# Attention scores and values accumulated in place by narrower matmuls, in a float32 decoder layer with compensated products

## The chip, the cores and the metric

The kernel runs on one core of one Trainium2 chip. The metric is the device time in microseconds of one execution. The core's engines run side by side, each with its own queue: TensorE (PE in the profile, with its weight loads as PEld), VectorE (DVE), ScalarE (ACT), GpSimd (POOL) and SyncE (SP), which here only starts transfers.

## The reference

A decoder layer for 256 tokens of 2048 channels in float32. The input is normalised and projected; one branch is causal attention with 16 heads and low-rank queries, keys and values, the other a short gated convolution; both are projected, merged by gates, projected once more and normalised. The part that the change touches is the attention:

```python
def one_block(args):
    qn, qr, blk = args                      # a block of 128 queries
    sc = (einsum('bqhd,bkhd->bhqk', qn, k_nope)
          + einsum('bqhr,bkr->bhqk', qr, k_rope)).astype(float32) * scale
    mask = key_pos[None, :] <= q_pos[:, None]
    sc = where(mask[None, None], sc, -inf)
    p = softmax(sc, axis=-1).astype(v.dtype)
    return einsum('bhqk,bkhd->bqhd', p, v)
...
attn = attn.reshape(b, s, MLA_WIDTH) * silu(z_mla)
```

A head has 128 channels without rotary position and 64 with, 128 value channels, 256 queries and keys.

## The kernel before, in words

Float32 products are made of two rounded parts each. An operand is split into a high part in the `fp32r` format (ScalarE copies it, `hi`) and the rest (VectorE subtracts, `lo`), which is `split_act`; a product is then hi x hi + hi x lo + lo x hi, three matmuls into one accumulator (`product`, `products`). Weights come from memory in units of 128 x 2048 (`raw`, three buffers), are split in halves of 1024 columns into `whi` and `wlo` (five buffers each), and are used by TensorE in a fixed order. Every matmul goes through a helper on line 88, so all matmuls have that line in the profile; they are told apart by the tiles they write and read.

The kernel has three stages: the latent products (`qa`, `ckv`, `kr`) up to about 50 us, the loop over 16 heads up to about 590 us, and the square products (`sq`, `sX`, `sY`, `sZ`, `out`) after it. In the loop over heads TensorE mostly works on the big input projections: `z` (the gates, `gates`) and `cv` (the convolution's four projections, `channels`), whose matmuls are 512 columns wide. Between their quarters the heads' own steps are put by hand: `group_a` and `group_r` make queries and keys for two heads (`qn`, `kn`, `qr`), `group_v` the values for four (`vv`), `score(h)` the scores, `turn` the transposed and split weights of the softmax (`pt`), and `values(h)` the weighted sum.

The order of all matmuls is pinned (`tc.keep_in_program_order`). The other engines' instructions are ordered by a planner that simulates a timeline, unless they are pinned too. Accumulators are banks of 128 x 512 float32: a ring of four with the tag `mm`, two with the tag `cv`, one `st`, one `o`.

*Scores before.* `sc` (bank `st`) holds the first block of 128 queries against the first 128 keys, `sw` (a bank `mm`) the second block against all 256. A matmul of the high query part multiplies the high and the low key part side by side in one instruction, so each bank has two halves: the left one collects hi x hi, lo x hi and the high part of the rotary product, the right one hi x lo and the low part of the rotary product (`qr` has its high and low part on the two halves of the partitions). Columns of the six matmuls: 256, 128, 256 for `sc`, and 512, 256, 512 for `sw`. `softmax` has ScalarE copy the two right halves out (`sc_half`, `half`, line 695), VectorE add them to the left ones (lines 698 and 700) and add the causal mask (lines 699 and 701). Then come maximum, exponential, sum and scaling, and a transpose through memory (`turned`: `far<-via` and back). With `behind`, which is given for every second head (`score(h + 1, later=True)`), the copies of line 695 are pinned.

*Values before.* `o` has two halves in the same way. One matmul of 512 columns stands ahead of a `yield`, at which the caller puts other steps, and three of 256, 128 and 256 behind it. `whole` (lines 433 and 434) has ScalarE copy the right half out and VectorE add it to the left; line 745 multiplies the sum into the gate `at`.

Of the kernel before, what the change touches and what calls it, by code (L numbers as in the profile page):

```python
# [14 lines left out]
AF = mybir.ActivationFunctionType  # L15
ALU = mybir.AluOpType
PSUM = bass.MemoryType.PSUM

P = 128
S = 256  # L20
NT = S // P
# [61 lines left out]
def tile_layer(ctx: ExitStack, tc: tile.TileContext, xw, w0, xb, x, pos, pvec, post_g, wc, wz, wcv, wkr, wqk, wqr, wv, cwr, wsq, out):  # L83
    nc = tc.nc
# [151 lines left out]
    def bank(name, tag="mm", bufs=4):  # L236
        return psum.tile([P, 512], F32, name=name, tag=tag, bufs=bufs)
# [94 lines left out]
    kr = bp.tile([P, 2, S], F32R, name="kr")  # L332
    mask = bp.tile([P, 3 * P], F32, name="mask")
# [12 lines left out]
    def temp(name, shape=(P, S), dt=F32, bufs=2, tag=None):  # L346

        tag, n = tag or name.rstrip("0123456789_"), shape[-1]
        if n % LINE == 0:
            return bp.tile(list(shape), dt, name=name, tag=tag, bufs=bufs)  # L350
        return bp.tile([P, -(-n // LINE) * LINE], dt, name=name, tag=tag, bufs=bufs)[:, :n]


    def turned(src, via, n, far=None, queue=nc.gpsimd):

        via = via[:, : P * n]
        v = via.rearrange("p (q k x) -> p q k x", q=4, k=n)
        nc.vector.transpose(v.rearrange("p q k x -> p k q x"), src)  # L358
        if far is None:
            far = dram.tile([P, P * n], F32, name="far", tag=f"far{n}", bufs=4)[:, :]  # L360

        def go():
            f = far.rearrange("(q y) (i m) -> i y q m", q=4, i=4)
            for i in range(4):
                m = via[32 * i : 32 * i + 32, :].rearrange("y (q m) -> y q m", q=4)
                tc.keep_in_program_order(queue.dma_start(out=f[i], in_=m))  # L366

        def come(dst):

            tc.keep_in_program_order(queue.dma_start(out=dst, in_=far))  # L370

        return go, come
# [57 lines left out]
    def whole(dst, ps):  # L430

        t = temp("half")
        nc.scalar.activation(t[:, :], ps[:, S:], AF.Copy)
        nc.vector.tensor_tensor(dst, ps[:, :S], t[:, :], op=ALU.add)
# [237 lines left out]
    def scores(h):  # L672

        (qn, kn), qr = groups["a", h // HG], groups["r", h // HG]
        j = h % HG
        sc, wide_sc = bank(f"sc{h}", tag="st", bufs=1), bank(f"sw{h}")
        t0, t1 = slice(0, P), slice(P, S)
        mm = matmul
        o = sc[:, :S].rearrange("p (i k) -> p i k", i=2)
        mm(o, qn[0][:, j, t0], kn[:, :, j, :P], start=True, stop=False)  # L680
        mm(sc[:, :P], qn[1][:, j, t0], kn[:, 0, j, :P], start=False, stop=False)
        mm(o, qr[:, j, t0], kr[:, :, :P], start=False, stop=True)
        o = wide_sc[:, :].rearrange("p (i k) -> p i k", i=2)
        mm(o, qn[0][:, j, t1], kn[:, :, j, :], start=True, stop=False)
        mm(wide_sc[:, :S], qn[1][:, j, t1], kn[:, 0, j, :], start=False, stop=False)
        mm(o, qr[:, j, t1], kr[:, :, :], start=False, stop=True)
        return lambda behind: softmax(h, sc, wide_sc, behind)

    def softmax(h, sc, wide_sc, behind):
        if h == 0:  # L690
            temp("pad", (P, 4 * LINE), bufs=1)
        p = temp("p", (P, 3 * P), bufs=2)
        half, wide_half = temp("sc_half", (P, P), bufs=1), temp("half")
        for dst, src in ((half, sc[:, P:S]), (wide_half, wide_sc[:, S:])):
            now = nc.scalar.activation(dst[:, :], src, AF.Copy)
            if behind:
                tc.keep_in_program_order(now)
        nc.vector.tensor_tensor(p[:, :P], sc[:, :P], half[:, :], op=ALU.add)
        nc.vector.tensor_tensor(p[:, :P], p[:, :P], mask[:, :P], op=ALU.add)
        nc.vector.tensor_tensor(p[:, P:], wide_sc[:, :S], wide_half[:, :], op=ALU.add)  # L700
        nc.vector.tensor_tensor(p[:, P:], p[:, P:], mask[:, P:], op=ALU.add)
        mx, sm, rs = temp("mx", (P, NT)), temp("sm", (P, NT)), temp("rs", (P, NT))
        nb = temp("nb", (P, NT))
        for t in range(NT):
            o = slice(t * P, (2 * t + 1) * P)
            nc.vector.reduce_max(mx[:, t : t + 1], p[:, o], axis=mybir.AxisListType.X)
        nc.vector.tensor_scalar(nb[:, :], mx[:, :], -SCALE, None, op0=ALU.mult)
        for t in range(NT):
            o = slice(t * P, (2 * t + 1) * P)
            nc.scalar.activation(  # L710
                p[:, o], p[:, o], AF.Exp, bias=nb[:, t : t + 1], scale=SCALE,
                accum_out=sm[:, t : t + 1],
            )
        nc.vector.reciprocal(rs[:, :], sm[:, :])
        for t in range(NT):
            o = slice(t * P, (2 * t + 1) * P)
            nc.vector.tensor_scalar(p[:, o], p[:, o], rs[:, t : t + 1], None, op0=ALU.mult)
        go, come = turned(p[:, :], temp("via", (P, 3 * P), bufs=1), 3)
        go()
        return p, lambda: come(p[:, :])  # L720

    def turn(p):

        pt = temp("pt", (P, 2, 3 * P), F32R, 1)
        hi, lo = (pt[:, j : j + 1, :].rearrange("p o (k q) -> p (o k) q", k=3) for j in range(2))
        split_act(quarters(hi), quarters(lo), by_rows(p[:, :], 3), True)
        return pt

    def values(h, pt):
        vv = groups["v", h // HV]  # L730
        j = h % HV
        o = bank(f"o{h}", tag="o", bufs=1)
        vs = slice(j * DV, (j + 1) * DV)
        both = o[:, :].rearrange("p (i q) -> p i q", i=2)
        mm = matmul
        mm(both, vv[0][:, 0, vs], pt[:, :, :S], start=True, stop=False)
        yield
        mm(o[:, :S], vv[1][:, 0, vs], pt[:, 0, :S], start=False, stop=False)
        mm(o[:, P:S], vv[1][:, 1, vs], pt[:, 0, S:], start=False, stop=False)
        mm(both[:, :, P:], vv[0][:, 1, vs], pt[:, :, S:], start=False, stop=True)  # L740

        at = at_t[:, h // HV, :, :].rearrange("p t (i k x) -> p t i k x", i=4, k=HV)[:, :, :, j, :]
        f = temp("f")
        whole(f[:, :], o)
        nc.vector.tensor_tensor(at, f[:, :].rearrange("p (t i x) -> p t i x", t=NT, i=4), at, op=ALU.mult)


    at_t = at_f[:, :, :].rearrange("p (v t k) s -> p v t (k s)", v=NV, t=NT)
# [188 lines left out]
    def score(h, later=False):  # L937
        made_here = scores(h)

        def rest():  # L940
            ps_by_head[h], come = made_here(later)
            coming.append(come)

        return rest if later else rest()
# [49 lines left out]
    for h in range(H):  # L994
        v, at = divmod(h, HV)
# [12 lines left out]
        if at == 0:  # L1008
            for i in range(4):
                gates(v, i)  # L1010
                if v == 0 and i == 0:
                    ckv_come()
                elif v == 0 and i == 1:
                    key_rope()
                elif v == 0 and i == 2:
                    latent_split("qa", qa, "q_g")
                elif v and i == 0:
                    arrive()
                elif v and i == 1:
                    pt = turn(ps_by_head.pop(h - 1))  # L1020
                elif v and i == 2:
                    o = values(h - 1, pt)
                    next(o)
                    finish_all(make("v", v))
                    score(h)
                    finish_all(o)
                elif v and i == 3:
                    next(tap)
            if not v:
                latent_split("ckv", ckv, "kv_g")  # L1030
            gates_done(v)
            if v:
                arrive()
# [23 lines left out]
        else:  # L1057
            pt = turn(ps_by_head.pop(h - 1))
# [19 lines left out]
        if at:  # L1078
            steps.append(values(h - 1, pt))
# [10 lines left out]
        if h == H - 1:  # L1090
            pt = turn(ps_by_head.pop(h))
# [70 lines left out]
    seq, pending, now = [], {}, [0]  # L1162
# [49 lines left out]
    def branch_block(c, both, n, combine):  # L1212

        sums_of[n, c] = []

        def last(pss):
            for t in range(NT):
                sums_of[n, c].append(pss[t])
                meet((n, c), t, combine)

        return block(c, n, lambda k: both[k // 4][:, k % 4, :], {}, last)
# [147 lines left out]
    p = [branch_block(c, at_b, 2, weigh) for c in range(4)]  # L1369
# [121 lines left out]
    op = ctx.enter_context(tc.tile_pool(name="op", bufs=1))  # L1491
# [177 lines left out]
```

## Time and profile before

| | |
|---|---|
| median of 3 runs | 1013.3 us (1013.11 to 1013.71) |
| span of the profiled execution | 1011.8 us, first to last instruction |
| its time outside the span | not listed; the runs' median is 1.5 us longer than the span |
| TensorE busy | 1004.2 us, 4552 matmuls and 4552 weight loads |
| VectorE busy | 811.4 us, 1111 instructions |
| ScalarE busy | 586.3 us, 838 instructions |
| GpSimd busy | 170.7 us, 311 instructions |
| transfers | 261.84 MB, mean 259 GB/s |
| mean granted TensorE clock | 0.998 |

The profile is one execution, recorded by the hardware. An engine's busy time is the union of its instructions; for matmuls, which overlap, the ends are modelled, so that consecutive starts tell more than lengths. The chain of waits is the work that ended last, followed back from the last instruction through whatever released each step. A row of the groups gives line, engine, operation, output and inputs, the shape, the count, the busy time, the mean length in ns, and the idle time of the engine ahead of them with what ended it.

### The profile page before, as it was taken

The numbers are of one execution on the slowest core, as the hardware profiler recorded it, in microseconds if no ns is written. First come the engines' busy times: TensorE is split into PE (matmuls) and PEld (weight loads), VectorE is DVE, ScalarE is ACT, GpSimd is POOL, SyncE is SP. The second block draws the span as 40 slices with busy tenths as digits, with TensorE's granted clock in tenths as the row PEclk, the third lists the DMA queues.
The fourth block names the chain that finished last, engine by engine and source line by source line (L and its number), as shares of the span: only waits on it lengthen the run. The fifth ranks groups of instructions, "written<-read, shape, count | busy, mean of one in ns | idle before, by whom it ended". The sixth has DMA issues, their size and how long they took to land.

```text
span 1011.8 us, 12983 instructions
## 1 busy us (share of the span) xinstructions
PE 1004.2 (99%) x4552; PEld 835.4 (83%) x4552; DVE 811.4 (80%) x1111; ACT 586.3 (58%) x838; POOL 170.7 (17%) x311
## 2 busy tenths in 40 slices
PE   9999999999999999999999999999999999999997
PEld 7888888888888888888888888888888888888886
DVE  7588878868888689877797889898989779997562
ACT  7675656556556456555565465565675664674541
POOL 4620411113211223212133110000000001003000
PEclk9999999999999999999999999999999999999999
DMA  8785768568786668866689779897599989639742
GB/s 338 282 291 183 260 201 304 197 214 276 234 303 232 228 229 283 272 219 232 216 264 338 292 306 291 344 375 218 187 333 296 305 321 260 239 127 322 289 166 84
DMA packets 54369, 261.84 MB, mean 259 GB/s; under 512 B 8768, under 2 KB 13504, under 8 KB 29216
## 3 DMA queue, kind: packets, MB, share of 16 engines
q1 hardware_dynamic: 37728, 214.35, 57.7%
q0 software_dynamic: 12256, 38.13, 14.0%
q10 hardware_dynamic: 4320, 8.54, 2.4%
q8 instruction: 35, 0.57, 0.2%
q14 instruction: 30, 0.25, 0.1%
HBM read 234.80 MB, written 22.02 MB: 254 GB/s over the span
## 4 chain that ended last, share of the span: by engine, by line
PE 98%; DMA 1%; DVE 0%; ACT 0%; SPq 0%; issue 0%
PE cv L88 34%; PE sq L88 17%; PE sX L88 9%; PE z L88 9%; PE out L88 9%; PE sZ L88 4%; PE kn L88 2%; PE qn L88 2%; PE vv L88 2%; PE sY L88 2%; PE ckv L88 2%; PE qa L88 2%; PE qr L88 1%; PE o L88 1%; PE sw L88 1%; DMA raw<-xb_dram 1%
## 5 line engine op out<-in xcount | busy, mean ns | idle before, releaser
L265 ACT ACTIVATE whi<-raw 128x1024 fp32r<-128x1024 f32 (+1 forms) x302 | 306.1, 1028 | 236.7 <-PE cv L88 103.9
L266 DVE TENSOR_TENSOR wlo<-raw,whi 128x1024 fp32r<-128x1024 f32 (+1 forms) x300 | 352.7, 1188 | 101.2 <-ACT whi L265 74.6
L88 PE MATMUL cv<-whi,x_both 128*128 128x512 f32 x1024 | 319.8, 389 | 0.0
L88 PEld LDWEIGHTS cv<-whi,x_both 128*128 128x128 f32 x1024 | 192.3, 188 | 39.5
L88 PE MATMUL cv<-wlo,x_both 128*128 128x512 f32 x512 | 199.5, 390 | 0.0
L88 PEld LDWEIGHTS cv<-wlo,x_both 128*128 128x128 f32 x512 | 96.2, 188 | 19.4
L266 DVE TENSOR_TENSOR slo_V<-b,shi_V 128x1024 fp32r<-128x1024 f32 x60 | 71.5, 1218 | 15.9 <-PE sq L88 8.5
L265 ACT ACTIVATE shi_V<-b 128x1024 fp32r<-128x1024 f32 x60 | 61.5, 1053 | 39.2 <-PE sq L88 21.2
L88 PE MATMUL z<-whi,x_both 128*128 128x512 f32 x256 | 80.0, 389 | 0.0
L366 POOL DMA_DIRECT2D far<-via x64 | 35.4, 559 | 227.2 <-DVE via L358 217.2
L88 PE MATMUL sq<-whi,at_both 128*128 128x512 f32 x256 | 60.6, 389 | 0.0
L88 PE MATMUL sq<-whi,cv_both 128*128 128x512 f32 x256 | 60.6, 389 | 0.0
L88 PEld LDWEIGHTS sq<-whi,cv_both 128*128 128x128 f32 x256 | 48.0, 188 | 10.0
L88 PEld LDWEIGHTS sq<-whi,at_both 128*128 128x128 f32 x256 | 48.0, 188 | 10.0
L88 PEld LDWEIGHTS z<-whi,x_both 128*128 128x128 f32 x256 | 48.1, 188 | 9.9
L88 PE MATMUL z<-wlo,x_both 128*128 128x512 f32 x128 | 49.8, 389 | 0.0
L88 PE MATMUL out<-whi,m_both 128*128 128x512 f32 x208 | 49.4, 389 | 0.0
L88 PE MATMUL sX<-shi_V,form 128*128 128x512 f32 x192 | 47.4, 389 | 0.0
L88 PEld LDWEIGHTS out<-whi,m_both 128*128 128x128 f32 x208 | 39.0, 188 | 8.1
L88 PEld LDWEIGHTS sX<-shi_V,form 128*128 128x128 f32 x192 | 36.0, 188 | 7.5
L265 ACT ACTIVATE shi_Q<-b 128x1024 fp32r<-128x1024 f32 x28 | 28.8, 1052 | 21.5 <-PE sq L88 19.1
L1263 POOL DMA_DIRECT2D b<-wsq_dram x8 | 7.0, 869 | 193.4 <-DVE b L1272 76.8
(304 smaller groups left out, 1568.7 us busy)
## 6 DMA issues: line engine op xcount, KB each, us to landing
raw<-wcv_dram SPq DMA_DIRECT2D x64, 1024.0 KB, 6.2
raw<-wsq_dram SPq DMA_DIRECT2D x48, 1024.0 KB, 7.2
b<-wsq_dram SPq DMA_DIRECT2D x26, 1024.0 KB, 5.7
raw<-wz_dram SPq DMA_DIRECT2D x16, 1024.0 KB, 4.9
raw<-wqk_dram SPq DMA_DIRECT2D x8, 1024.0 KB, 6.8
b<-wsq_dram POOLq DMA_DIRECT2D x8, 1024.0 KB, 11.0
far_form<-form ACTq DMA_DIRECT2D x28, 256.0 KB, 3.3
form<-far_form SPq DMA_DIRECT2D x7, 1024.0 KB, 13.8
```

The costliest lines, as they stand in the source:

```text
L88: return tc.keep_in_program_order(nc.tensor.matmul(*a, **kw))
L265: a = nc.scalar.activation(hi, src, AF.Copy)
L266: b = nc.vector.tensor_tensor(lo, src, hi.bitcast(F32), op=ALU.subtract)
L366: tc.keep_in_program_order(queue.dma_start(out=f[i], in_=m))
L1263: tc.keep_in_program_order(nc.gpsimd.dma_start(out=dst[:, :], in_=wsq[n, c + b, k], accum_op=ALU.add))
```

## The change

The scores of a head go into one bank, `sc` alone: columns 0 to 127 for the first block of queries, 128 to 383 for the second. The high and the low key part are multiplied by two matmuls that accumulate in the same columns, five matmuls of 128 columns for the first block and five of 256 for the second, so the bank holds the whole score, laid out as the mask is. ScalarE's two copies and VectorE's two additions of halves go, and one addition of the mask over 384 columns, reading the bank, takes the place of two; it is this addition that is pinned with `behind`. The values are accumulated in the left half of `o` by six matmuls: two of 256 columns ahead of the `yield`, and 256, 128, 128 and 128 behind it. `whole` is not called there any more, and the product with the gate reads the bank. No transfer is added or removed.

```diff
 
         (qn, kn), qr = groups["a", h // HG], groups["r", h // HG]
         j = h % HG
-        sc, wide_sc = bank(f"sc{h}", tag="st", bufs=1), bank(f"sw{h}")
-        t0, t1 = slice(0, P), slice(P, S)
+        sc = bank(f"sc{h}", tag="st", bufs=1)
         mm = matmul
-        o = sc[:, :S].rearrange("p (i k) -> p i k", i=2)
-        mm(o, qn[0][:, j, t0], kn[:, :, j, :P], start=True, stop=False)
-        mm(sc[:, :P], qn[1][:, j, t0], kn[:, 0, j, :P], start=False, stop=False)
-        mm(o, qr[:, j, t0], kr[:, :, :P], start=False, stop=True)
-        o = wide_sc[:, :].rearrange("p (i k) -> p i k", i=2)
-        mm(o, qn[0][:, j, t1], kn[:, :, j, :], start=True, stop=False)
-        mm(wide_sc[:, :S], qn[1][:, j, t1], kn[:, 0, j, :], start=False, stop=False)
-        mm(o, qr[:, j, t1], kr[:, :, :], start=False, stop=True)
-        return lambda behind: softmax(h, sc, wide_sc, behind)
-
-    def softmax(h, sc, wide_sc, behind):
+        for t, o in ((0, sc[:, :P]), (1, sc[:, P : 3 * P])):
+            q, keys = slice(t * P, (t + 1) * P), slice(0, (t + 1) * P)
+            mm(o, qn[0][:, j, q], kn[:, 0, j, keys], start=True, stop=False)
+            mm(o, qn[0][:, j, q], kn[:, 1, j, keys], start=False, stop=False)
+            mm(o, qn[1][:, j, q], kn[:, 0, j, keys], start=False, stop=False)
+            mm(o, qr[:, j, q], kr[:, 0, keys], start=False, stop=False)
+            mm(o, qr[:, j, q], kr[:, 1, keys], start=False, stop=True)
+        return lambda behind: softmax(h, sc, behind)
+
+    def softmax(h, sc, behind):
         if h == 0:
             temp("pad", (P, 4 * LINE), bufs=1)
         p = temp("p", (P, 3 * P), bufs=2)
-        half, wide_half = temp("sc_half", (P, P), bufs=1), temp("half")
-        for dst, src in ((half, sc[:, P:S]), (wide_half, wide_sc[:, S:])):
-            now = nc.scalar.activation(dst[:, :], src, AF.Copy)
-            if behind:
-                tc.keep_in_program_order(now)
-        nc.vector.tensor_tensor(p[:, :P], sc[:, :P], half[:, :], op=ALU.add)
-        nc.vector.tensor_tensor(p[:, :P], p[:, :P], mask[:, :P], op=ALU.add)
-        nc.vector.tensor_tensor(p[:, P:], wide_sc[:, :S], wide_half[:, :], op=ALU.add)
-        nc.vector.tensor_tensor(p[:, P:], p[:, P:], mask[:, P:], op=ALU.add)
+        now = nc.vector.tensor_tensor(p[:, :], sc[:, : 3 * P], mask[:, :], op=ALU.add)
+        if behind:
+            tc.keep_in_program_order(now)
         mx, sm, rs = temp("mx", (P, NT)), temp("sm", (P, NT)), temp("rs", (P, NT))
         nb = temp("nb", (P, NT))
         for t in range(NT):
@@ -731,18 +723,17 @@
         j = h % HV
         o = bank(f"o{h}", tag="o", bufs=1)
         vs = slice(j * DV, (j + 1) * DV)
-        both = o[:, :].rearrange("p (i q) -> p i q", i=2)
         mm = matmul
-        mm(both, vv[0][:, 0, vs], pt[:, :, :S], start=True, stop=False)
+        mm(o[:, :S], vv[0][:, 0, vs], pt[:, 0, :S], start=True, stop=False)
+        mm(o[:, :S], vv[0][:, 0, vs], pt[:, 1, :S], start=False, stop=False)
         yield
         mm(o[:, :S], vv[1][:, 0, vs], pt[:, 0, :S], start=False, stop=False)
-        mm(o[:, P:S], vv[1][:, 1, vs], pt[:, 0, S:], start=False, stop=False)
-        mm(both[:, :, P:], vv[0][:, 1, vs], pt[:, :, S:], start=False, stop=True)
+        mm(o[:, P:S], vv[0][:, 1, vs], pt[:, 0, S:], start=False, stop=False)
+        mm(o[:, P:S], vv[0][:, 1, vs], pt[:, 1, S:], start=False, stop=False)
+        mm(o[:, P:S], vv[1][:, 1, vs], pt[:, 0, S:], start=False, stop=True)
 
         at = at_t[:, h // HV, :, :].rearrange("p t (i k x) -> p t i k x", i=4, k=HV)[:, :, :, j, :]
-        f = temp("f")
-        whole(f[:, :], o)
-        nc.vector.tensor_tensor(at, f[:, :].rearrange("p (t i x) -> p t i x", t=NT, i=4), at, op=ALU.mult)
+        nc.vector.tensor_tensor(at, o[:, :S].rearrange("p (t i x) -> p t i x", t=NT, i=4), at, op=ALU.mult)
 
 
     at_t = at_f[:, :, :].rearrange("p (v t k) s -> p v t (k s)", v=NV, t=NT)
```

## The prediction

> **What bounds the kernel now.** I read four views in this order: the page's busy shares and chain, the waits of TensorE alone, one attention stretch in windows, and then the timeline of TensorE matmul by matmul. First the page and the waits whose waiting engine is TensorE (columns: who waited, for whom, total us, times, longest):
>
> ```profile
> PE 1004.2 (99%) x4552; PEld 835.4 (83%) x4552; DVE 811.4 (80%) x1111; ACT 586.3 (58%) x838; POOL 170.7 (17%) x311
> PE 98%; DMA 1%; DVE 0%; ACT 0%; SPq 0%; issue 0%
> ```
> ```profile
> PE fin L88 <- ACT dg L1541: 0.9, 1, 0.9
> PE idle L88 <- PEq L1657: 0.8, 1, 0.8
> PE qa L88 <- ACT whi L265: 0.6, 2, 0.3
> ```
> ```profile
> 12.00:575.00 563.00, 563.00 (x2610) 470.99 (x2609) 451.05 (x760) 331.92 (x540) 140.24 (x251) 1.00 0.74 256
> ```
>
> TensorE's matmuls carry 98% of the chain that ends last. In the whole program TensorE is recorded waiting for others for 2.3 us, at the first product (`qa`), in the warm-up (`idle`) and in the very last product (`fin`); none of these belongs to a head. In the window from 12 to 575 us (columns: length, then busy of PE, PEld, DVE, ACT, POOL, granted clock, DMA share, GB/s) PE is busy for all 563.00 us at a granted clock of 1.00. But a busy PE need not be a PE at its own pace, since the ends of matmuls are modelled. So the starts must be read. The chain of waits gives the pace of wide matmuls (start, length, count), and two timelines give the heads:
>
> ```profile
> 106.86 21.77 PE cv L88 x96
> ```
> ```profile
> 92.33 0.39 PE L88 MATMUL cv<-whi,x_both 128*128 128x512 f32 x1
> 92.55 0.28 PE L88 MATMUL sc<-kn,qn_hi 128*128 128x256 f32 x1
> 92.67 0.22 PE L88 MATMUL sc<-kn,qn_lo 128*128 128x128 f32 x1
> 92.73 0.34 PE L88 MATMUL sc<-kr,qr 128*128 128x256 f32 x1
> 92.90 0.39 PE L88 MATMUL sw<-kn,qn_hi 128*128 128x512 f32 x1
> 93.13 0.28 PE L88 MATMUL sw<-kn,qn_lo 128*128 128x256 f32 x1
> 93.25 0.39 PE L88 MATMUL sw<-kr,qr 128*128 128x512 f32 x1
> 93.47 0.40 PE L88 MATMUL cv<-whi,x_both 128*128 128x512 f32 x1
> ```
> ```profile
> 92.56 0.19 PEld L88 LDWEIGHTS sc<-kn,qn_lo 128*128 128x128 f32 x1
> 92.67 0.19 PEld L88 LDWEIGHTS sc<-kr,qr 128*128 128x128 f32 x1
> 92.78 0.19 PEld L88 LDWEIGHTS sw<-kn,qn_hi 128*128 128x128 f32 x1
> 92.90 0.19 PEld L88 LDWEIGHTS sw<-kn,qn_lo 128*128 128x128 f32 x1
> ```
> ```profile
> 185.63 0.39 PE L88 MATMUL o<-pt,vv_hi 128*128 128x512 f32 x1
> 185.85 0.34 PE L88 MATMUL o<-pt,vv_lo 128*128 128x256 f32 x2
> 186.03 0.34 PE L88 MATMUL o<-pt,vv_hi 128*128 128x256 f32 x1
> 186.20 1.11 PE L88 MATMUL qn<-qa,wlo 128*128 128x256 f32 x8
> 187.15 1.12 PE L88 MATMUL kn<-ckv,wlo 128*128 128x256 f32 x8
> 188.11 0.40 PE L88 MATMUL cv<-whi,x_both 128*128 128x512 f32 x1
> ```
>
> A 512-wide matmul takes 21.77 / 96 = 0.227 us of the engine. A head's six score matmuls run from 92.55 to 93.47, 0.92 us, and its four value matmuls 0.22 us (the wide one) and 0.35 us (185.85 to 186.20). 256-wide matmuls that follow one another take 0.95 / 8 and 0.96 / 8, so 0.119 to 0.120 us.
>
> The reader should look at the one narrow matmul of the scores. The 128-wide one starts at 92.67 and the next at 92.73, as if it cost 0.06. But the 256-wide one behind it then holds its place for 0.17 (92.73 to 92.90) and is recorded 0.06 longer than the other 256-wide one of the same tile (0.34 against 0.28). The rows of the weight loads say why: the loads at 92.56, 92.67, 92.78 and 92.90 are 0.11 to 0.12 apart, and each matmul has one (4552 of each). The third load could not start before the matmul of the second one really began, at 92.78 and not at 92.73. So a load takes a slot of about 0.115 us. A matmul of 256 columns or more covers the next load, one of 128 columns does not, and costs the slot of a 256-wide one: the two together take 92.67 to 92.90, 0.23 us. The head's narrow matmuls are bound by loads, not by columns.
>
> **The change part by part.** *Scores, TensorE.* Six matmuls become ten. The columns stay 1920 (256 + 128 + 256 + 512 + 256 + 512 before; five of 128 and five of 256 after), so by columns nothing changes. By load slots it does: five 128-wide and five 256-wide matmuls each fill a slot. The first of a narrow stretch takes 0.113 to 0.12 (92.55 to 92.67), the later ones 0.119 by the rows of eight. I take 0.113 + 9 x 0.119 = 1.184 us against 0.92: +0.262 us for a head. No row shows two 128-wide matmuls in a row; the pair above is the nearest, and the bounds below are for that.
>
> *Values, TensorE.* Ahead of the `yield`, one 512-wide becomes two 256-wide: 0.113 + 0.119 against 0.227, +0.005. Behind it 256, 128 and 256 (two strided pieces) become 256, 128, 128, 128: 0.113 + 3 x 0.119 = 0.470 against 0.35, more exactly 0.344 (the narrow pair at 0.23 and the first at 0.113): +0.126. Together +0.131.
>
> Sum on TensorE: (0.262 + 0.131) x 16 heads = 6.3 us. It all lies on the path, since TensorE waits for nothing there. With every slot at 0.113 it is (0.21 + 0.00 + 0.11) x 16 = 5.1 us. With every slot at 0.121 it is (0.288 + 0.015 + 0.140) x 16 = 7.1 us. There may be something more: behind a narrow stretch the wide matmuls take a few ns longer (93.47 starts a 0.40 one, 0.39 is usual). Estimated at 0.02 us for each of 32 stretches, that adds up to 0.7 us, so the upper end is 7.8.
>
> *ScalarE and VectorE.* The rows by form (count, busy us, mean ns, idle before):
>
> ```profile
> L695 ACT ACTIVATE half<-sw 128x256 f32<-128x256 f32 x16 | 6.1, 380 | 0.0
> L433 ACT ACTIVATE half<-o 128x256 f32<-128x256 f32 x16 | 6.0, 377 | 5.9 <-PE o L88 5.9
> L695 ACT ACTIVATE sc_half<-sc 128x128 f32<-128x128 f32 x16 | 4.2, 262 | 0.0
> L434 DVE TENSOR_TENSOR f<-o,half 128x256 f32<-128x256 f32 x16 | 6.7, 420 | 14.5 <-ACT half L433 14.5
> L701 DVE TENSOR_TENSOR p<-p,mask 128x256 f32<-128x256 f32 x16 | 6.7, 417 | 0.1
> L700 DVE TENSOR_TENSOR p<-sw,half 128x256 f32<-128x256 f32 x16 | 6.6, 413 | 0.0
> L698 DVE TENSOR_TENSOR p<-sc,sc_half 128x128 f32<-128x128 f32 x16 | 4.6, 284 | 0.1
> L699 DVE TENSOR_TENSOR p<-p,mask 128x128 f32<-128x128 f32 x16 | 4.5, 281 | 0.1
> ```
>
> ACT loses 380 + 262 + 377 ns a head, 16.3 us in all. DVE loses 284 + 281 + 413 + 417 + 420 ns and gets one 128x384 addition. From 284 at 128 and 413 at 256 columns it is estimated at 413 + 129 = 542 ns. So DVE loses 1273 ns a head, 20.4 us in all. The product into `at_f` stays, now with PSUM as its first source, at about the 420 ns of `f<-o,half`, which has the same shape and reads PSUM too. I put all of this at 0 us of the span: these engines work beside TensorE, which waits for them nowhere between 12 and 575 us. What gets earlier is the softmax of a head and with it POOL's `far<-via` transfer. What is late next after it is TensorE's own program order, which does not move. No DMA is added, removed or moved past another.
>
> *The bank.* A head no longer takes one of the four `mm` banks for `sw`, so the other users of that ring find their bank free no later than before: 0, as they do not wait now.
>
> *The new waits.* The mask addition and the product into `at_f` now make VectorE itself wait for TensorE, where ScalarE waited. Behind them on VectorE stand the `wlo` splits that TensorE consumes. The rows of waits that show the size and the cover:
>
> ```profile
> ACT whi L265 <- PE cv L88: 103.9, 78, 3.6
> DVE f L434 <- ACT half L433: 14.5, 8, 3.0
> ACT half L433 <- PE o L88: 5.9, 4, 4.9
> ```
>
> The longest wait for `o` was 4.9 us. The splits stand ahead so far that ScalarE waits 78 times for TensorE to free a buffer: five buffers of 1024 columns, each feeding 12 matmuls, are 5 x 12 x 0.227 = 13.6 us of work. Up to 4.9 us hides in that. If the cover were gone, it would cost 4.9 us for each such wait.
>
> Sum: +6.3 us on TensorE, nothing back. The span of the profiled execution is 1011.8 us and its slots make the sum: 1011.8 + 6.3 = 1018.1 of span. The runs' median lies 1.5 us above that span (1013.3), which the change does not touch: 1019.6 us.
>
> **The rivals.** *A 128-wide matmul costs its columns.* If the 0.06 between starts at 92.67 and 92.73 were its true price, and the 0.17 behind it belonged to the strided 256-wide matmul for some other reason, then scores would take 5 x 0.060 + 5 x 0.119 = 0.895, values 0.232 and 0.119 + 3 x 0.060 = 0.299. That is 0.067 us less than now for a head, 1.1 us in all: 1012.2 us, no slower. With a price of x ns the head changes by -67 + 8(x - 60) ns; zero at 68, and above the 0.2% from x = 84. Against it stand the load starts 0.11 apart. The Trainium skill ("TensorE: Matmul & The Clock Gate", section "Back-to-back issue gap") gives about 81 ns per matmul for a sustained stream of load and matmul pairs at 128 columns. By that the sum would be +1.6 us, 1014.9, and the change could not be told from none. The trace does not agree: the only narrow matmul here and its follower take 0.23 us together, which leaves the narrow one 0.115. And for 512 columns the same section has 131 ns where 96 of them here took 227 ns each. I give this rival 5 in 100.
>
> *Repeated weights are not loaded again.* The new order puts six pairs with the same stationary operand next to each other in each head (`qn[0]` and `qr` in both query blocks, `vv[0]` of both key blocks). If the second load were dropped, a pair of 128-wide matmuls would cover the next load as one 256-wide does now, and the time would stay within 0.5 us: 1013.5. The count of loads now equals that of matmuls, but the only repeated operand, the warm-up's, is in a format that splits each matmul into two passes, so its 16 loads for 8 matmuls decide nothing. 4 in 100.
>
> *VectorE's wait takes the place of ScalarE's and reaches TensorE.* The planner places the unpinned instructions anew; if a mask addition or a product is put so early that VectorE stands longer than the 13.6 us of splits last, or stands there where the splits are short, TensorE waits. One wait of 4.9 us with no cover gives 1024.5. For it: VectorE is 80% busy and idles 14.5 us already ahead of `f<-o`. Against it: it gets 20 us lighter, and TensorE does not wait once there now. 5 in 100.
>
> **How the numbers follow.** 86 in 100 for the load-slot forecast, 5.1 to 7.8 us more (1018.4 to 1021.1), with 1019.6 the likeliest. 0.2%, 2.0 us, is about what a measurement of this kernel can tell from no change. The first two rivals end within it (0.09, of which 0.01 may be faster by more); the forecast and the third are slower (0.91). The range that leaves out no more than 2 in 10 is the forecast's own, with some room for the price of rows of 128-wide matmuls: 1018.0 to 1021.5.
>
> **What would show it.** In the changed kernel the score matmuls of a head should take about 1.18 us from the first start to the next product's, the five 128-wide ones about 0.119 each with loads as far apart; the value matmuls 0.23 and 0.47. TensorE should have 4648 matmuls and loads, 96 more, and still no wait between 12 and 575 us. ACT's busy time should fall by 16 us and DVE's by 20 us, and the stage behind the heads should be moved later by some 6 us and not be longer. The prediction is wrong if 128-wide matmuls in a row start 0.06 to 0.08 apart, if the loads are fewer than the matmuls, or if TensorE is recorded waiting for a `wlo` split inside a head.

## The result, and the profile after

The changed kernel takes 1019.21 us (median of 4, 1018.62 to 1019.59) against 1013.5 us beside it: a ratio of 1.0058, 95% interval 1.0046 to 1.0070. It is slower by 5.7 us; the forecast was 1019.6. The profiled execution has a span of 1017.8 us, 6.0 more than before.

The page's busy shares and chain:

```profile
PE 1010.4 (99%) x4648; PEld 843.5 (83%) x4648; DVE 795.4 (78%) x1047; ACT 575.5 (57%) x790; POOL 170.1 (17%) x311
PE 94%; DMA 2%; DVE 2%; ACT 1%; issue 0%; SPq 0%; DVEq 0%; ACTq 0%
```

There are 96 matmuls and 96 loads more, one load for each matmul as before; VectorE and ScalarE are lighter. The waits of TensorE alone:

```profile
PE fin L88 <- ACT dg L1532: 0.9, 1, 0.9
PE idle L88 <- PEq L1648: 0.8, 1, 0.8
PE qa L88 <- ACT whi L265: 0.4, 1, 0.4
```

No wait belongs to a head. The 6 us must be in the pace. A stage is best bounded by its first matmuls: `ckv` opens the stage with the heads' loop in it, `sX` the one behind. From the timeline of TensorE, first before and then after:

```profile
27.52 0.84 PE L88 MATMUL ckv<-whi,x_both 128*128 128x512 f32 x3
...
589.91 2.02 PE L88 MATMUL sX<-whi,form 128*128 128x512 f32 x8
```
```profile
27.44 0.84 PE L88 MATMUL ckv<-whi,x_both 128*128 128x512 f32 x3
...
595.61 2.06 PE L88 MATMUL sX<-whi,form 128*128 128x512 f32 x8
```

The stage took 562.39 us and takes 568.17: +5.78 us. Below, "the heads' stage" is always this stretch. Now a head's scores and the loads of their weights, in the timeline (start, length, line, output and inputs, shape, count):

```profile
92.48 0.33 PE L88 MATMUL sc<-kn,qn_hi 128*128 128x128 f32 x2
92.65 0.27 PE L88 MATMUL sc<-kn,qn_lo 128*128 128x128 f32 x1
92.76 0.38 PE L88 MATMUL sc<-kr,qr 128*128 128x128 f32 x2
92.98 0.45 PE L88 MATMUL sc<-kn,qn_hi 128*128 128x256 f32 x2
93.27 0.28 PE L88 MATMUL sc<-kn,qn_lo 128*128 128x256 f32 x1
93.39 0.40 PE L88 MATMUL sc<-kr,qr 128*128 128x256 f32 x2
93.62 0.40 PE L88 MATMUL cv<-whi,x_both 128*128 128x512 f32 x1
```
```profile
92.59 0.19 PEld L88 LDWEIGHTS sc<-kn,qn_lo 128*128 128x128 f32 x1
92.70 0.30 PEld L88 LDWEIGHTS sc<-kr,qr 128*128 128x128 f32 x2
92.92 0.30 PEld L88 LDWEIGHTS sc<-kn,qn_hi 128*128 128x128 f32 x2
93.16 0.19 PEld L88 LDWEIGHTS sc<-kn,qn_lo 128*128 128x128 f32 x1
```

The scores run from 92.48 to 93.62, 1.14 us against 0.92. The loads of the 128-wide part are 0.11 apart (92.59, 92.70, and two until 92.92), those of the 256-wide part 0.12 (two from 92.92 to 93.16). The first interval of the matmuls, 92.48 to 92.65 for two, looks short for the reason seen before: a matmul behind a 128-wide one is recorded some 0.06 before its weights are there. The values of a head, again from the timeline:

```profile
186.81 0.40 PE L88 MATMUL o<-pt,vv_hi 128*128 128x256 f32 x2
187.04 0.28 PE L88 MATMUL o<-pt,vv_lo 128*128 128x256 f32 x1
187.16 0.34 PE L88 MATMUL o<-pt,vv_hi 128*128 128x128 f32 x2
187.34 0.27 PE L88 MATMUL o<-pt,vv_lo 128*128 128x128 f32 x1
187.45 1.16 PE L88 MATMUL qn<-qa,wlo 128*128 128x256 f32 x8
188.45 1.12 PE L88 MATMUL kn<-ckv,wlo 128*128 128x256 f32 x8
```

0.23 for the first two, 0.41 for the four behind the `yield`, and 0.05 more in the eight matmuls of `qn` that follow (1.00 against 0.95), where the last load's exposed part is recorded.

Summed over all heads from start to next start, the 5.78 us are: scores 14.75 to 18.36 us (+3.62), values 9.16 to 10.18 (+1.02), `qn`, `kn` and `qr` +0.54, the 512-wide `cv` and `z` +0.52, the rest 0.08. Of the 0.52 about half, 0.24 us, is in the five wide matmuls that stand right behind values, 0.05 each, which fits the exposed load seen in `qn`.

The two spans are 6.04 us apart, so 0.26 us more lie outside that stage. One part is the stage behind it, from the first `sX` to the first `fin` matmul: 413.99 us against 413.48. The chain of waits shows where (start, length, what). `far_cv<-mv` is a transfer to memory, `raw<-wsq_dram` the load of a unit of weights, `whi` and `wlo` its split:

```profile
610.62 3.01 DMA far_cv<-mv
...
614.19 12.72 DMA raw<-wsq_dram
...
627.02 1.07 ACT whi L265
...
629.25 0.79 DVE first_rt L1263
...
631.45 1.23 DVE wlo L266
...
632.73 1.43 PE sq L88 x5
```

A unit of weights lands at 626.9, the low part of its second half is made only at 631.45, behind an addition of VectorE (`first_rt`), and TensorE's starts there fall 0.41 us behind their pace. The list of waits does not have it, since the modelled ends cover it; the chain has, and the distances between starts. The start and the very end were together 0.24 us shorter.

### The profile page after: what moved, and what is told of

Same layout as the page of the kernel before. It is cut to its first block, busy times and chain, and to the rows that moved or that the text cites. A ratio compares the mean times of both kernels' runs of the same rounds, so it can differ in the third digit from the quotient of the medians.

```text
span 1017.8 us, 13049 instructions
## 1 busy us (share of the span) xinstructions
PE 1010.4 (99%) x4648; PEld 843.5 (83%) x4648; DVE 795.4 (78%) x1047; ACT 575.5 (57%) x790; POOL 170.1 (17%) x311
## 4 chain that ended last, share of the span: by engine, by line
PE 94%; DMA 2%; DVE 2%; ACT 1%; issue 0%; SPq 0%; DVEq 0%; ACTq 0%
PE cv L88 34%; PE sq L88 15%; PE z L88 9%; PE out L88 9%; PE sX L88 8%; PE sZ L88 4%; PE qa L88 2%; PE qn L88 2%; PE kn L88 2%; PE vv L88 2%; PE sY L88 2%; PE ckv L88 2%; PE sc L88 2%; DMA raw<-wsq_dram 1%; PE qr L88 1%; PE o L88 1%
```

## The experiments

The theory is that a matmul narrower than 256 columns costs the slot of its weight load, so the time goes by slots and not by columns, and that the relief of ScalarE and VectorE is worth nothing. The rivals: the columns decide, and the time comes from waits that the planner's new order brings; the relief is worth something; repeated weights are cheaper; the slot is a floor of any matmul and not the load.

**Scores alone.** `softmax` and `scores` of the changed kernel, `values` of the one before.

> Only the scores of the change, with the mask addition; the values as before. Load-slot theory (a matmul of 128 columns costs what one of 256 does): ten slots against 0.92 us now, by the changed kernel's rows 1.146 us a head, so 0.225 x 16 = +3.6 us, 1.0036 of before. Column theory (the columns decide, and the rest of the 6 us is made by new waits): 0 us, 1.000. Planner theory (a wait that the new order brings): anything, with TensorE recorded waiting inside the heads.

Measured: 1.0037 of before (1.0025 to 1.0050), heads' stage 566.26 us, +3.87.

**Values alone.** The opposite.

> Only the values of the change; scores and softmax as before. Load-slot theory: +0.005 us ahead of the yield and about 0.113 behind it, x 16 = +1.9 us, 1.0019 of before; together with the scores alone this makes the whole change. Column theory: 0 us, 1.000. Planner theory: the two parts need not add up to the whole.

Measured: 1.0019 (1.0010 to 1.0028), heads' stage 564.30 us, +1.91. The two parts make 3.87 + 1.91 = 5.78 us, the whole change to within 0.01 us. Accidents of the planner would hardly add up so.

**First block 256 wide.**

```diff
-        for t, o in ((0, sc[:, :P]), (1, sc[:, P : 3 * P])):
-            q, keys = slice(t * P, (t + 1) * P), slice(0, (t + 1) * P)
+        for t, o in ((0, sc[:, :S]), (1, sc[:, P : 3 * P])):
+            q, keys = slice(t * P, (t + 1) * P), slice(0, S)
```

> The changed kernel, with the five score matmuls of the first query block 256 columns wide instead of 128 (the columns beyond 128 are overwritten by the second block). Load-slot theory: the slot is there already, at most 5 x 0.007 x 16 = +0.6 us over the changed kernel, so +6.0 to +6.6 us and 1.006 of before. Column theory: 5 x 0.053 x 16 = +4.3 us over the changed kernel, 1.010 of before.

Measured: 1.0066 (1.0053 to 1.0079), heads' stage 568.91 us, 0.74 more than the changed kernel. 640 columns a head were added and cost 0.046 us a head. The column theory's 4.3 us are out of reach. The timeline of its scores:

```profile
92.69 0.40 PE L88 MATMUL sc<-kn,qn_hi 128*128 128x256 f32 x2
92.92 0.28 PE L88 MATMUL sc<-kn,qn_lo 128*128 128x256 f32 x1
93.04 0.40 PE L88 MATMUL sc<-kr,qr 128*128 128x256 f32 x2
93.28 0.40 PE L88 MATMUL sc<-kn,qn_hi 128*128 128x256 f32 x2
```

From 92.69 to 93.28 are five matmuls at 0.118, where the 128-wide ones take 0.11.

**First block mostly 64 wide.** Four of the five matmuls get half the keys.

```diff
+            if t == 0:
+                o, keys = sc[:, : P // 2], slice(0, P // 2)
```

> The changed kernel, with four of the five score matmuls of the first query block only 64 columns wide (half of these keys get only the first product). Load-slot theory: a load's slot stays, the same time as the changed kernel within 0.3 us, 1.006 of before. Column theory: 4 x 0.027 x 16 = 1.7 us less than the changed kernel, 1.004.

Measured: 1.0064 (1.0052 to 1.0077), heads' stage 568.22 us, 0.05 more than the changed kernel. Half the columns gave nothing back. So from 64 to 256 columns a matmul costs about the same.

**Five 128-wide matmuls more.** The first block's scores once more, into the bank's unused columns.

```diff
-        for t, o in ((0, sc[:, :P]), (1, sc[:, P : 3 * P])):
+        for t, o in ((0, sc[:, :P]), (0, sc[:, 3 * P :]), (1, sc[:, P : 3 * P])):
```

> The changed kernel, with the five 128-wide score matmuls of the first query block done once more into the unused columns of the bank. This prices a 128-wide matmul: load-slot theory 5 x 0.112 x 16 = +9.0 us over the changed kernel, 1.0147 of before; column theory 5 x 0.057 x 16 = +4.5 us, 1.010; 81 ns each +6.5 us, 1.012.

Measured: 1.0142 (1.0128 to 1.0156), heads' stage 576.78 us. 8.61 us for 80 matmuls are 0.108 us for one. Its timeline, from the first of the five to the matmul behind them:

```profile
92.26 0.39 PE L88 MATMUL sc<-kn,qn_hi 128*128 128x128 f32 x2
92.49 0.28 PE L88 MATMUL sc<-kn,qn_lo 128*128 128x128 f32 x1
92.60 0.39 PE L88 MATMUL sc<-kr,qr 128*128 128x128 f32 x2
92.82 0.45 PE L88 MATMUL sc<-kn,qn_hi 128*128 128x256 f32 x2
```

Five matmuls from 92.26 to 92.82 are 0.112 each; over all heads the score rows grew by 8.94 us, while the wide matmuls took some 0.3 us less in this run. So the price by itself is 0.108 to 0.112; 0.057 and 0.081 are excluded by the interval, since they would give 1.010 and 1.012.

**The same five, with half the weights to load.** The five extra matmuls have a stationary operand of 64 columns.

```diff
+        for t, o in ((0, sc[:, :P]), (2, sc[: P // 2, 3 * P :]), (1, sc[:, P : 3 * P])):
...
+            if t == 2:
+                q, keys = slice(0, P // 2), slice(0, P)
```

> The changed kernel with five more 128-wide matmuls a head into unused columns of the bank, as in the run with five more, but with a stationary operand of 64 columns instead of 128 (queries 0 to 63). This asks whether the slot of 0.108 to 0.112 us is the load of the weights or a floor of any matmul. If it is the load, and a load takes time by the columns it loads: 5 x 0.057 x 16 = +4.6 us over the changed kernel, 1.0105 of before. If it is a floor of a matmul, or a load takes the same time whatever its columns: +8.6 us as with 128, 1.0142.

Measured: 1.0098 (1.0083 to 1.0113), heads' stage 572.96 us: 4.79 us for 80 matmuls, 0.060 for one. Its timeline, matmuls and loads:

```profile
92.34 0.29 PE L88 MATMUL sc<-kn,qn_hi 128*64 128x128 f32 x2
92.46 0.22 PE L88 MATMUL sc<-kn,qn_lo 128*64 128x128 f32 x1
92.52 0.28 PE L88 MATMUL sc<-kr,qr 128*64 128x128 f32 x2
92.64 0.45 PE L88 MATMUL sc<-kn,qn_hi 128*128 128x256 f32 x2
```
```profile
92.28 0.20 PEld L88 LDWEIGHTS sc<-kn,qn_hi 128*64 128x64 f32 x2
92.40 0.14 PEld L88 LDWEIGHTS sc<-kn,qn_lo 128*64 128x64 f32 x1
92.47 0.19 PEld L88 LDWEIGHTS sc<-kr,qr 128*64 128x64 f32 x2
92.59 0.30 PEld L88 LDWEIGHTS sc<-kn,qn_hi 128*128 128x128 f32 x2
```

The five go from 92.34 to 92.64, 0.060 apart, and so do their loads. The same 128 moving columns cost 0.108 with 128 weights' columns and 0.060 with 64. So the slot goes by the columns of the weights, as a load does, and is no floor of a matmul. Two limits: 0.060 is also about what 128 moving columns take by the 512-wide ones (0.227 / 4 = 0.057), so it bounds a load of 64 columns from above only; and with 64 columns of weights only 64 rows of the bank are written, which no run took apart from the load. That it is the load is argued from the load starts, which keep the same distances, and not shown apart from that. The Trainium skill ("TensorE: Matmul & The Clock Gate", section "LDWEIGHTS (loading the stationary operand)") has a load's time go by the columns of the stationary operand, columns / 1.2 in ns; by that an estimate is 107 ns for 128 columns, and the 0.108 measured agrees.

**No equal neighbours.** The order within a block becomes `qn[0]`, `qr`, `qn[1]`, `qn[0]`, `qr`.

> The changed kernel, with the order of the five score matmuls of a block changed so that no two neighbours have the same stationary operand. Load-slot theory: the same, 1.006 of before, since every matmul loads its weights anyway. If repeated weights made a load cheaper: up to 4 slots a head more, up to 4 x 0.057 x 16 = +3.6 us over the changed kernel.

Measured: 1.0063 (1.0049 to 1.0076), heads' stage 568.14 us against 568.17. Whether the same weights come twice in a row makes no difference in the scores.

**The relief without the narrow matmuls.** Matmuls of before, mask addition directly from the banks, no `whole` for the values.

```diff
+        now = nc.vector.tensor_tensor(p[:, :P], sc[:, :P], mask[:, :P], op=ALU.add)
...
+        now = nc.vector.tensor_tensor(p[:, P:], wide_sc[:, :S], mask[:, P:], op=ALU.add)
...
+        nc.vector.tensor_tensor(at, o[:, :S].rearrange("p (t i x) -> p t i x", t=NT, i=4), at, op=ALU.mult)
```

> The matmuls of the kernel before, with the lighter work of the change on ScalarE and VectorE: the right halves of the banks (the low parts of keys, rotary keys and softmax weights) are left out of the result, so no copies and no additions of halves. Load-slot theory with TensorE as the only bound: 0 us, 1.000 of before, though ACT falls by some 16 us of busy time and DVE by some 20. If the lighter engines are worth something that the narrow matmuls then hide: faster, up to what TensorE's slow starts between 12 and 1000 us hold, about 2 us, 0.998.

Measured: 0.9999 (0.9990 to 1.0008), heads' stage 562.41 us against 562.39. The relief alone is worth nothing here, to within 0.1%.

**The narrow matmuls without the relief.**

```diff
+        for dst, src in ((half, sc[:, :P]), (wide_half, sc[:, P : 3 * P])):
+            now = nc.scalar.activation(dst[:, :], src, AF.Copy)
...
+        nc.scalar.activation(half[:, :], o[:, :S], AF.Copy)
+        nc.vector.tensor_tensor(f[:, :], o[:, :S], half[:, :], op=ALU.add)
```

> The matmuls of the changed kernel, with the heavier work of before put back on ScalarE and VectorE (two copies and four additions for a softmax, a copy and an addition for the values; the values are added to their own copy, so the scores and values are doubled). Load-slot theory: +6 us, 1.006 of before, as the changed kernel: the relief was worth nothing. If the relief paid part of the cost: slower than the changed kernel, by 0.5 us or more.

Measured: 1.0075 (1.0063 to 1.0088), heads' stage 568.08 us, 0.09 less than the changed kernel. In the stage where the work stands it costs nothing. The whole time is another matter: the ratio's middle is 1.7 us above the changed kernel's, though the two intervals overlap, and the median of 1020.63 us is 1.2 to 1.5 above the runs with the first block mostly 64 wide and without equal neighbours, which were measured beside it (1019.43 and 1019.09). The profile has 0.4 us of it, behind the heads: 414.40 us from `sX` to `fin` against 413.99. But the profiled execution, at 1019.56, was the quickest of the five (the others 1020.19 to 1021.88), so no trace shows the rest. Whether the relief saves up to some 1.7 us outside the heads stays open.

**The changed kernel again.**

> The changed kernel unaltered, for the comparison with the others: load-slot theory +5.8 us from the heads' slots, 1.0057 of before; its wait of some 0.4 us at 632 us of the span may be there or not.

Measured: 1019.26 us, 1.0057 (1.0044 to 1.0070), heads' stage 568.14 us. The stage from `sX` to `fin` took 414.56 us this time: TensorE falls behind at two places there, by some 0.45 us each, of which the list of waits has 0.2 each. Over the profiles that stage took 413.48 in the two kernels with the matmuls of before and 413.56 to 414.56 in those with changed ones, up to 1.1 us more, and 0.6 us apart for the very same kernel. With the values alone, with half the weights and without equal neighbours it was at most 0.11 us longer than before, so the narrow matmuls as such do not make it longer. In four profiles (this kernel's two, the first block 256 wide, and the one without the relief) TensorE falls behind at the change of stages, where a unit of weights is split late; with five more matmuls it does so at another place, near 789 us. Which of the shifted transfers makes a unit late was not tried.

## Why the prediction was right

- *What bounds.* In the heads TensorE's slots, and no wait: shown by the two runs with the relief taken alone and taken away, whose heads' stages are within 0.1 us of the kernels with the same matmuls.
- *Scores.* +0.262 us a head forecast, 0.226 measured in their own rows (0.242 by the run with the scores alone, which has what they do to their neighbours). The term is too large because I took 0.119 for every narrow matmul from rows of 256-wide ones. A 128-wide one costs 0.108 to 0.112; the 256-wide ones are the slower ones. Five of them at some 0.007 less are 0.035 us a head, all but 0.001 of the difference.
- *Values.* +0.131 forecast; 0.064 in their own rows and 0.034 (0.54 / 16) in the eight or four matmuls behind them, some 0.10; the run with the values alone gives 0.119. Three 128-wide slots at 0.007 less are 0.02 of the difference.
- *Slower wide matmuls behind a narrow stretch.* Named as up to 0.7 us and left out of the middle: `cv` and `z` took 0.52 us more. But it is not what was named, some ns at each of 32 stretches: 0.24 us is the exposed load behind values in five places, and some 0.2 us is spread over the 1800 wide matmuls further off. The reason given, a recorded length of 0.40 us against 0.39, was a modelled one.
- *Sum.* 6.3 forecast, 5.78 in the heads' stage. Scores and values were forecast 1.1 us too high by their own rows and `qn`, `kn` and `qr`; what was left out of the middle gave back 0.6. That the forecast of the whole came as close as 0.4 us is luck on top, since the stage behind gave 0.5 us to the other side.
- *The stage behind the heads should not be longer.* This failed, by 0.51 us in the first profile and 1.08 in the second. "What is late next is TensorE's own program order" left out the units of weights that are loaded and split at the change of stages.
- *ACT less by 16 us, DVE by 20.* It was 586.3 - 575.5 = 10.8 and 811.4 - 795.4 = 16.0. The mask addition over 384 columns and the product reading the bank came as estimated:

```profile
L691 DVE TENSOR_TENSOR p<-sc,mask 128x384 f32<-128x384 f32 x16 | 8.8, 551 | 0.1
L736 DVE TENSOR_TENSOR at_f<-o,at_f 128x256 f32<-128x256 f32 x16 | 6.7, 420 | 9.1 <-PE o L88 8.6
```

  551 ns against 542, 420 against 420. What I took out was too large: I added lengths of instructions that overlap. In the timelines of before, of VectorE and of ScalarE:

```profile
114.23 0.29 DVE L698 TENSOR_TENSOR p<-sc,sc_half 128x128 f32<-128x128 f32 x1
114.44 0.42 DVE L700 TENSOR_TENSOR p<-sw,half 128x256 f32<-128x256 f32 x1
```
```profile
113.40 0.27 ACT L695 ACTIVATE sc_half<-sc 128x128 f32<-128x128 f32 x1
113.55 0.39 ACT L695 ACTIVATE half<-sw 128x256 f32<-128x256 f32 x1
```

  The next one starts 0.21 us behind a first of 0.29, and 0.15 behind one of 0.27. As with matmuls, starts tell the cost.
- *The rivals.* A price by columns: excluded by five more matmuls at 0.108. So is a price of 81 ns, which the Trainium skill ("TensorE: Matmul & The Clock Gate", section "Back-to-back issue gap") has for 128 columns; the trace does not agree. The prediction's working of the first has a slip: by its own terms the price by columns makes 0.065 us a head less, 1.0 us in all, and not 0.067 and 1.1, which changes nothing. Repeated weights not loaded again: excluded by 4648 loads and by the order without equal neighbours. VectorE's new wait for `o` is there (8.6 us before the product, in the row above, where ScalarE waited 5.9 before) and reaches no matmul of a head.

## What to carry to other kernels

On an engine that runs at its own pace, count the slots: what fits the rows here is that a matmul takes the longer of its moving columns (0.227 us for 512) and the load of the next weights (0.108 to 0.112 us for 128 columns). So a load of 128 columns hides behind 256 moving columns (0.118 to 0.120 us) and not behind 128. A 512-wide matmul cut in two costs next to nothing (0.227 to 0.23 us ahead of the `yield`), but a 256-wide one cut into two of 128 costs almost a whole slot more. And before work is taken off an engine, see in the waits whether anything ever stood still for it: 96 more matmuls bought 27 us of busy time on two engines for which TensorE did not wait in a head.

## What the runs showed of the hardware that was not expected

128-wide matmuls in a row are a little faster than 256-wide ones in a row, 0.108 to 0.112 us against 0.118 to 0.120, although both stand at one load each. A matmul of 64 columns with a full load costs as much as one of 128 (heads' stages 0.05 us apart with 64 such), while 128 columns with a load of half the weights took 0.060 us. And a wait of TensorE of 0.4 us can be absent from the list of its waits and its busy share, and show only in the starts and in the chain.
